# Two of 22 down-projection chunks as whole float32 products in a hybrid encoder trunk

## The chip, the cores and the metric

The kernel runs on one core of a Trainium2 chip, in one launch. The metric is the device time of an execution in microseconds; where several executions were timed, it is their median. The kernel before took 907.94 us, the median of three runs from 906.53 to 909.02 us.

## What is computed

The reference is a trunk of two macaron layers over 256 tokens of width 1024, all in float32. Each layer has a feed-forward network (FFN), a mixer (an mLSTM in the first layer, a windowed attention in the second) and a second FFN, each followed by a layer norm:

```python
def swiglu(x, w_in, w_out):
    gu = x @ w_in
    g, u = gu[..., :D_FF], gu[..., D_FF:]
    return (jax.nn.silu(g) * u) @ w_out

for l in range(DEPTH):                                   # DEPTH = 2
    x = layer_norm(ALPHA * x + 0.5 * swiglu(x, ffn_w_in[l, 0], ffn_w_out[l, 0]), ...)
    y = mlstm_mixer(x, ...) if l % 2 == 0 else window_attention(x, ...)
    x = layer_norm(ALPHA * x + y, ...)
    x = layer_norm(ALPHA * x + 0.5 * swiglu(x, ffn_w_in[l, 1], ffn_w_out[l, 1]), ...)
```

`D_FF` is 2816, so the hidden vector h = silu(g) * u of an FFN is 22 chunks of 128 features, and the down product h @ w_out is a sum over these 22 chunks.

## The kernel before

**Split operands.** Nearly every matmul runs on operands of type float32r. A weight tile of 128 x 1024 float32 arrives by DMA as a word (`w_raw`, or `s_raw` for sums of blocks). ScalarE casts it to a high part (`w_hi`, in `Weights.high`, L299), VectorE subtracts that from the word for a low part (`w_lo`, in `Weights.low`). Activations are split likewise (`h_hi`, `h_lo`; `xT`). A product is then three parts: high by high, low by high and high by low (`HH`, `LH`, `HL`, `mm_by`). VectorE, ScalarE and TensorE thus all have a share of each word.

**An FFN.** Chunks 0 to 3 of h come from wide products and are turned by TensorE transposes (`tr`, L817), which write to a PSUM bank and are read from there by ScalarE and VectorE. Chunks 4 and 5 come from narrow products that have the weights as the standing operand, so that their h lies turned already, in `v[1]`, a tile of 128 x 512 float32. `turn` splits it into `hp[0]` (ScalarE) and `hp[1]` (VectorE). Chunks 6 to 21 come from four runs of `seven` (L973), which forms two by two blocks with seven products instead of eight and needs sums of weight blocks for that.

**The down product.** `down(n)` (L942) takes the next n words of w_out and adds their chunk to four PSUM banks, y[t][o], two blocks of 128 tokens by two halves of 512 columns. A chunk is twelve matmuls of 512 columns: three parts by four banks. In the first run of `seven`, chunk 4 follows the product with S4, and chunk 5 the product after it.

**What sets the order.** TensorE's order is the order of the program text. What VectorE and ScalarE do between is set by `Paced`, a recording layer that keeps a clock for each engine from simple costs, and by `Weights.fill` (L375), which splits the next words whenever these clocks say that VectorE or ScalarE is idle. `Paced.on_tensor` (L160) counts a float32 matmul as two passes. Loads stand in SyncE's queue in the order in which `Weights.load` (L222) issued them; a load needs a free room. There are four rooms of the tag `w_raw` and one more inside an FFN, and a room comes free when the word's low part has been made (`Weights.drop`, L260). Up to ten high and ten low parts are kept (`RING`).

**The mLSTM.** After the projections of q and k come, for each of four heads, `scores` (L1230; VectorE weighs the scores in `wt`, ScalarE casts them to `a_hi`, VectorE makes `a_lo`) and, one head later, `mix` (L1249), whose first matmul needs `a_hi`. Between them stand products for the output gate with eight words, taken at once by `W.take(8)` (L1321). Ahead of that, `W.done(most=1 if m and g else 2)` (L1223) lets one more word be split.

Of the kernel before, what the change touches and what calls it, by code (L numbers as in the profile page):

```python
# [9 lines left out]
F32 = mybir.dt.float32  # L10
# [32 lines left out]
PEND = [6, 4, 6, 6, 6]  # L43


AHEAD = 300.0
URGENT = 3
SOON = -1000.0
# [139 lines left out]
class Weights:  # L188
# [110 lines left out]
    def high(self, i):  # L299

        nc = self.nc
        p = self.plan[i]
        while self.half and (p["word"] not in self.raw or any(h[0] == p["needs"] for h in self.half)):
            self.low()
        while any(s_[0] == p["needs"] or p["word"] not in self.raw for s_ in self.sums):
            self.sum()
        if p["word"] not in self.raw:
            return False
        scale, raw = p["scale"], self.raw[p["word"]]
        hi = self.pool.tile([128, D], FR, name="w_hi", tag="w_hi", bufs=RING)  # L310
        if i == 0:
            for j in range(2):
                s_ = slice(j * 512, j * 512 + 512)
                nc.scalar.copy(hi[:, s_], raw[:, s_])
        elif scale is None:
            nc.scalar.copy(hi, raw)
        else:
            nc.scalar.activation(hi, raw, AF.Copy, scale=scale())
        self.half.append((i, hi))
        self.made.add(i)  # L320
        return True
# [82 lines left out]
    def take(self, n):  # L404
# [2 lines left out]
        self.split(self.used)  # L407
        return [self.parts[j] for j in range(i, i + n)]

    def take_rows(self, n):  # L410
        return [(self.used + j, w) for j, w in enumerate(self.take(n), -n)]

# [34 lines left out]
def trunk_kernel(ctx: ExitStack, tc: tile.TileContext, x, ffn_w_in, ffn_w_out, ln_g, ln_b, ml_w_in, ml_gate_b,  # L447
# [17 lines left out]

    clock = [0.0]

    def split_of(w, scale=None, needs=None, takes=2720.0, behind=0.0):

        plan.append(dict(word=w, k=words[w]["k"], scale=scale, needs=needs, due=clock[0], behind=behind))  # L470
        clock[0] += takes
        return len(plan) - 1

# [12 lines left out]
    def rows(w, c, scale=None):  # L486
        piece(w[c * 128:(c + 1) * 128, :].rearrange("(k p) f -> p k f", p=128), 1, scale)
# [36 lines left out]
    for j, (kind, l, i, _) in enumerate(stages):  # L524
        if kind == "ffn":
            wi, wo = ffn_w_in[l, i], ffn_w_out[l, i]
            nth = iter(range(2 * UNITS))

            def down(n):
                for _ in range(n):  # L530
                    rows(wo, next(nth))

            for c0 in (0, F):
                for a in range(4):
                    wide(wi, a * 256, c0)
            for c0 in (512, F + 512):
                for a in range(2):
                    narrow(wi, a * 512, c0)
            down(2)
            for g in range(SEVENS):  # L540
                c0 = 768 + 512 * g
                seven(wi, c0, F + c0, g, down)
            down(6)
        elif kind == "mlstm":
            for c0 in (1024, 1536):
                for a in range(4):
                    wide(ml_w_in[0], a * 256, c0)
            for c0 in range(0, 1024, 256):
                for a in range(2):
                    narrow(ml_w_in[0], a * 512, c0)  # L550
            for c0 in (2048, 2560):
                for a in range(4):
                    wide(ml_w_in[0], a * 256, c0)
            for c in range(8):
                rows(ml_w_out[0], c, (lambda c=c: gcol[:, c:c + 1]))
        else:
            for c0 in (1024, 0):
                for a in range(4):
                    wide(at_w_in[0], a * 256, c0)
            for c0 in (512, 768):  # L560
                for a in range(2):
                    narrow(at_w_in[0], a * 512, c0)
            for c in range(8):
                rows(at_w_out[0], c)
        ends[j] = len(words)
# [86 lines left out]
    def wbank(shape=(128, 512)):  # L652
        return psum.tile(list(shape), F32, name="pw", tag="pw", bufs=4)
# [143 lines left out]
    def ffn(l, i, n, pending, last):  # L797
        with ExitStack() as ph:
# [15 lines left out]
                warm(8)  # L814
            hs, pieces = [], []

            def tr(hB, t, h):  # L817
                p = wbank((128, 4, 128))
                for k in range(4):
                    nc.tensor.transpose(p[:, k], h[:, k * 128:(k + 1) * 128], ident)  # L820
                split_evac(pair(hB, A, A, tok(t)), p, wait=True)
# [120 lines left out]
            def down(n_):  # L942
                if not y:
                    y.extend([ybank() for _ in range(2)] for _ in range(2))
                W.flush()
                for _ in range(n_):
                    c = done_[0]
                    w, = W.take(1)
                    mm_by([((0, 1), [HH, LH]), ((2, 3), [HH]), ((0, 1, 2, 3), [HL]), ((2, 3), [LH])],
                          [(y[t][o], pair(hT[c], A, tok(t)), pair(w, A, 0, slice(o * 512, o * 512 + 512)), c == 0, False)  # L950
                           for t in range(2) for o in range(2)])
                    W.done()
                    done_[0] += 1
# [88 lines left out]
            for m in range(2):  # L1042
                p = [wbank((128, 2, S)) for _ in range(2)]
                for a in range(2):
                    w, = W.take(1)
                    for c in range(2):
                        for k in range(4):
                            nc.tensor.matmul(p[c], w[0][:, k, tok(c)], x_both[:, :, 4 * a + k], start=a == k == 0,
                                             stop=False)
                    for c in range(2):  # L1050
                        for k in range(4):
                            nc.tensor.matmul(p[c][:, 1], w[1][:, k, tok(c)], xT[0][:, 4 * a + k], start=False,
                                             stop=a == 1 and k == 3)
                        if a:
                            summed(p[c], v[m], c)
                    W.done()
                    if not start:
                        for n_, f_ in zip(XP[1:], (x_three, x_two, x_four)):
                            if 2 * m + a == n_:
                                f_()  # L1060
                    if m and not a:
                        W.flush()
                        for t in range(0 if start else 1, 2):
                            tr(hB0, t, hs[t])
                        nc.scalar.activation(v[0], v[0], AF.Silu)
            W.when_ready(lambda: nc.vector.tensor_mul(v[1], v[0], v[1]))
            chunks(hp, 2)
            down(1)

            def turn():  # L1070
                W.flush()
                nc.scalar.copy(hp[0], v[1])
                W.when_ready(lambda: nc.vector.tensor_sub(hp[1], v[1], hp[0].bitcast(F32)), hp[0])

            down(1)
            for g in range(SEVENS):
# [12 lines left out]
    def mlstm(l, n, pending, last):  # L1089
        with ExitStack() as ph:  # L1090
# [121 lines left out]
            for m in range(2):  # L1212
                for g in range(2):
                    pieces = W.take(2)
                    for f in range(2):
                        p = wbank((128, 2, S))
                        for k in range(8):
                            mm_both(p, pair(pieces[k // 4], A, k % 4, tok(f)), k, k == 0, k == 7)
                        if m == g == f == 0:
                            turn_gates()  # L1220
                        split_both(pair(held["qk"[m]], A, 2 * g + f), p, 128 ** -0.5 if m else 1.0,
                                   tile_([128, S], F32, "left"))
                    W.done(most=1 if m and g else 2)  # L1223
                    weights(2 * m + g)
                    W.done(0, 0 if m and g else 1)

# [91 lines left out]

            pump = iter(MP)
            spare = lambda: W.done(0, next(pump))  # L1320
            pieces = W.take(8)  # L1321
            po = [wbank(), wbank()]
            for h in range(4):
                wide_mm(po[h // 2], 0, pieces, h // 2, range(4 * (h % 2), 4 * (h % 2) + 4))
                if h > 1:
                    spare()
                scores(h, (lambda: combine(h - 2)) if h > 1 else None)
                if h == 0:
                    nc.scalar.preload_act_table(AF.Sigmoid)
                if h == 3:  # L1330
                    held.clear()
                    wt.clear()
                    for tag in TAGS[1:]:
                        W.back(tag, S_RAW)
                if h:
                    mix(h - 1)
                    divide(h - 1, (lambda: settle(h - 2)) if h > 1 else None)
                if h > 1:
                    spare()
# [299 lines left out]
```

## Time and profile before

| | us |
|---|---|
| median of three runs (lowest, highest) | 907.94 (906.53, 909.02) |
| the profiled execution's own time | 907.99 |
| its span, from the first to the last instruction | 906.2 |
| TensorE busy | 895.4 |
| VectorE busy | 809.3 |
| ScalarE busy | 573.0 |
| GpSimd busy | 144.1 |

The profiled execution is one run; 1.8 us of its time lie around the span. A row of a group gives the line, the engine (PE is TensorE, DVE VectorE, ACT ScalarE, POOL GpSimd, SP SyncE, with a q for an engine's queue), the operation, the output and inputs by their names in the program, the shapes, the count, the busy time and the mean length of one in nanoseconds, then the idle time ahead of them and what ended it. For a matmul the moving operand stands first behind the arrow and the standing one second. Nearly all instructions show line 179, the recording layer's call, so that groups are told by their tiles. Matmuls overlap: their starts are measured, their ends modelled.

### The profile page before, as it was taken

How to read it: one execution, taken by the hardware profiler on the slowest of the kernel's cores; microseconds unless marked ns; L12 is line 12 of the kernel's file. 1: busy time of each engine (PE TensorE's matmuls, PEld its weight loads, DVE VectorE, ACT ScalarE, POOL GpSimd, SP SyncE). 2: the span in 40 equal slices, each digit the busy share in tenths (PEclk: the TensorE clock that was granted, in tenths of full speed). 3: DMA queues.
4: the chain of work that ended last, by engine and by line, in shares of the span. 5: the costliest groups of instructions: out<-in, count | busy, mean ns of one | idle time of the engine just before them, and what ended most of it. 6: DMA issues, size and time to landing. Idle time of an engine off the chain costs nothing.

```text
span 906.2 us, 12409 instructions
## 1 busy us (share of the span) xinstructions
PE 895.4 (99%) x4403; PEld 748.5 (83%) x4403; DVE 809.3 (89%) x995; ACT 573.0 (63%) x798; POOL 144.1 (16%) x177
## 2 busy tenths in 40 slices
PE   9999999999999999999999999999999999999996
PEld 8888888888888888888888888888887788888885
DVE  5999999878799899999988999998867899899985
ACT  4876777447664666767636676765568566676760
POOL 0111113113221011211111112110413110111110
PEclk9999999999999999999999999999999999999998
DMA  8999998545637889998868899987333687999851
GB/s 280 356 291 292 309 258 213 186 141 165 225 94 243 321 213 243 298 265 248 242 203 288 216 279 289 281 212 231 120 112 117 238 274 241 226 300 265 244 140 46
DMA packets 100477, 208.53 MB, mean 230 GB/s; under 512 B 6664, under 2 KB 21040, under 8 KB 100416
## 3 DMA queue, kind: packets, MB, share of 16 engines
q1 hardware_dynamic: 82112, 173.04, 54.7%
q0 software_dynamic: 17728, 33.66, 22.4%
q10 hardware_dynamic: 576, 1.05, 0.4%
q8 instruction: 34, 0.56, 0.3%
q14 instruction: 27, 0.22, 0.1%
HBM read 206.65 MB, written 1.05 MB: 229 GB/s over the span
## 4 chain that ended last, share of the span: by engine, by line
PE 90%; DVE 4%; DMA 2%; issue 2%; ACT 2%; DVEq 0%; POOL 0%; POOLq 0%
PE pw L179 54%; PE py L179 35%; DVE w_lo L179 2%; DMA w_raw<-in_ml_w_in_dram 1%; DMA w_raw<-in_ffn_w_in_dram 1%; ACT w_hi L179 1%; DVE scan L179 1%; ACT wt L179 0%; DVE x L179 0%; DMA both_rows<-both_rows 0%; DVE left L179 0%; DVE stats L179 0%; DVE S_lo L179 0%; DVE s_raw L179 0%; DVE S L179 0%
## 5 line engine op out<-in xcount | busy, mean ns | idle before, releaser
L179 DVE TENSOR_TENSOR w_lo<-w_raw,w_hi 128x1024 fp32r<-128x1024 f32 (+1 forms) x213 | 255.5, 1219 | 20.2 <-ACT w_hi L179 18.7
L179 ACT CAST w_hi<-w_raw 128x1024 fp32r<-128x1024 f32 (+1 forms) x213 | 219.0, 1050 | 70.0 <-DMA w_raw<-in_ffn_w_in_dram 18.3
L179 DVE TENSOR_TENSOR w_lo<-s_raw,w_hi 128x1024 fp32r<-128x1024 f32 x192 | 228.8, 1217 | 12.2 <-ACT w_hi L179 12.2
L179 ACT CAST w_hi<-s_raw 128x1024 fp32r<-128x1024 f32 x192 | 196.2, 1053 | 66.1 <-DVE s_raw L179 41.5
L179 PE MATMUL pw<-w_hi,xT 128*128 128x512 f32 x832 | 236.8, 393 | 0.0
L179 PEld LDWEIGHTS pw<-w_hi,xT 128*128 128x128 f32 x832 | 154.5, 188 | 31.2 <-DVE xT L179 0.3
L120 POOL DMA_DIRECT2D s_raw<-in_ffn_w_in_dram x64 | 77.4, 1209 | 484.0 <-DVE s_raw L179 211.1
L179 PE MATMUL pw<-w_lo,xT 128*128 128x512 f32 x416 | 136.1, 390 | 0.0
L179 PE MATMUL py<-w_hi,h_hi 128*128 128x512 f32 x349 | 117.3, 396 | 0.0
L179 PE MATMUL py<-w_hi,h_lo 128*128 128x512 f32 x349 | 115.3, 390 | 0.0
L179 PE MATMUL py<-w_lo,h_hi 128*128 128x512 f32 x349 | 104.8, 390 | 0.0
L179 PEld LDWEIGHTS pw<-w_lo,xT 128*128 128x128 f32 x416 | 78.1, 188 | 16.3
L179 PE MATMUL pw<-w_lo,S_hi 128*128 128x512 f32 x256 | 78.8, 389 | 0.0
L179 PE MATMUL pw<-w_hi,S_hi 128*128 128x512 f32 x256 | 78.8, 389 | 0.0
L179 PE MATMUL pw<-w_hi,S_lo 128*128 128x512 f32 x256 | 78.8, 389 | 0.0
L179 DVE TENSOR_TENSOR s_raw<-s_raw,s_raw 128x1024 f32<-128x1024 f32 x64 | 76.8, 1219 | 0.5
L179 PEld LDWEIGHTS py<-w_hi,h_lo 128*128 128x128 f32 x349 | 65.5, 188 | 14.0
L179 PEld LDWEIGHTS py<-w_lo,h_hi 128*128 128x128 f32 x349 | 65.6, 188 | 13.5
L179 PEld LDWEIGHTS py<-w_hi,h_hi 128*128 128x128 f32 x349 | 64.4, 188 | 12.2
L179 ACT COPY e<-pw 128x512 f32<-128x512 f32 (+1 forms) x64 | 33.7, 534 | 37.5 <-PE pw L179 36.8
L179 PEld LDWEIGHTS pw<-w_hi,S_hi 128*128 128x128 f32 x256 | 48.1, 188 | 10.0
L179 PEld LDWEIGHTS pw<-w_lo,S_hi 128*128 128x128 f32 x256 | 48.1, 188 | 10.0
(197 smaller groups left out, 1065.6 us busy)
## 6 DMA issues: line engine op xcount, KB each, us to landing
s_raw<-in_ffn_w_in_dram SPq DMA_DIRECT2D x96, 512.0 KB, 8.0
w_raw<-in_ffn_w_out_dram SPq DMA_DIRECT2D x88, 512.0 KB, 6.3
w_raw<-in_ffn_w_in_dram SPq DMA_DIRECT2D x80, 512.0 KB, 5.8
s_raw<-in_ffn_w_in_dram POOLq DMA_DIRECT2D x64, 512.0 KB, 8.1
w_raw<-in_ml_w_in_dram SPq DMA_DIRECT2D x24, 512.0 KB, 4.6
w_raw<-in_at_w_in_dram SPq DMA_DIRECT2D x12, 512.0 KB, 4.5
w_raw<-in_ml_w_out_dram SPq DMA_DIRECT2D x8, 512.0 KB, 3.9
w_raw<-in_at_w_out_dram SPq DMA_DIRECT2D x8, 512.0 KB, 3.4
```

The lines of the kernel that those rows point to most:

```text
L120: self.nc.gpsimd.dma_start(ap, source, accum_op=OP.add)
L179: r = f(out, *args, **kw)
```

## The change

The change does four things.

- **Chunks 4 and 5 in one product.** `WHOLE = (4, 5)` names them. Their words are not split; the raw word itself is the moving operand, and h stays one float32 tile, written by VectorE's multiplication straight into the room of `hp[0]`. A chunk is now four matmuls with float32 operands. The split of h in `turn` is gone. The word's room comes free only when these four matmuls are done.
- **Two transposes' banks.** In the first FFN the two calls of `tr` inside the narrow products take their bank from the `py` banks, not from the `pw` banks.
- **A word's split.** In the mLSTM, `W.done` ahead of the last head's weights splits no word (`most=0`), and of the eight words for the output gate seven are taken at first and the eighth behind the first call of `scores`.
- **Bookkeeping** for these: `take_whole`, a field `whole` in the plan.

```diff
@@ Weights.high
+        if p["whole"]:
+            self.parts[i] = raw
+            self.made.add(i)
+            return True
@@ Weights
+    def take_whole(self):
+        w, = self.take(1)
+        return self.plan[self.used - 1]["word"], w
@@ ffn: tr
-            def tr(hB, t, h):
-                p = wbank((128, 4, 128))
+            def tr(hB, t, h, bank=wbank):
+                p = bank((128, 4, 128))
@@ ffn: down
+                    if c in WHOLE:
+                        i, w = W.take_whole()
+                        for t in range(2):
+                            for o in range(2):
+                                nc.tensor.matmul(y[t][o], whole[:, c - WHOLE[0], tok(t)], w[:, o * 512:o * 512 + 512],
+                                                 start=False, stop=False)
+                        W.drop(i)
+                        W.load()
+                        W.done()
+                        done_[0] += 1
+                        continue
@@ ffn: narrow products
-                            tr(hB0, t, hs[t])
+                            tr(hB0, t, hs[t], ybank if start else wbank)
-            W.when_ready(lambda: nc.vector.tensor_mul(v[1], v[0], v[1]))
+            whole = hp[0].bitcast(F32)
+            W.when_ready(lambda: nc.vector.tensor_mul(whole, v[0], v[1]))
@@ ffn: turn
-                nc.scalar.copy(hp[0], v[1])
-                W.when_ready(lambda: nc.vector.tensor_sub(hp[1], v[1], hp[0].bitcast(F32)), hp[0])
@@ mlstm
-                    W.done(most=1 if m and g else 2)
+                    W.done(most=0 if m and g else 2)
@@ mlstm
-            pieces = W.take(8)
+            pieces = W.take(7)
...
                 scores(h, (lambda: combine(h - 2)) if h > 1 else None)
+                if h == 0:
+                    pieces.extend(W.take(1))
```

On TensorE, in the first FFN, this is the place from the end of the product with S4 over chunk 4 to the product behind it, before:

```order
L179 MATMUL pw<-w_lo,S_hi 128x512 x2
L179 MATMUL py<-w_hi,h_hi 128x512 x2
L179 MATMUL py<-w_hi,h_lo 128x512 x2
L179 MATMUL py<-w_hi,h_hi 128x512 x2
L179 MATMUL py<-w_lo,h_hi 128x512 x4
L179 MATMUL py<-w_hi,h_lo 128x512 x2
L179 MATMUL pw<-w_hi,xT 128x512 x4
```

The same place after the change, on to chunk 5 (`h_hi` is now the room that holds the whole h):

```order
L180 MATMUL pw<-w_lo,S_hi 128x512 x2
L180 MATMUL py<-w_raw,h_hi 128x512 x4
L180 MATMUL pw<-w_hi,xT 128x512 x4
L180 MATMUL pw<-w_lo,xT 128x512 x2
L180 MATMUL pw<-w_hi,xT 128x512 x4
L180 MATMUL pw<-w_lo,xT 128x512 x2
L180 MATMUL pw<-ident,e_674 128x128 x4
L180 MATMUL py<-w_raw,h_hi 128x512 x4
```

Twelve instructions became four for each of the two chunks; nothing else moved on this engine.

On VectorE, in the mLSTM, these rows lead from the last head's k to the second head's scores, before:

```order
L179 SCALAR_TENSOR_TENSOR k_lo<-pw,left 128x256
L179 TENSOR_TENSOR w_lo<-w_raw,w_hi 128x1024
L179 TENSOR_TENSOR wt<-pw,wt 128x2x256
L179 TENSOR_TENSOR wt<-pw,wt 128x2x128
L179 TENSOR_TENSOR a_lo<-wt,a_hi 128x768
L179 TENSOR_TENSOR wt<-pw,wt 128x2x256
```

And after:

```order
L180 SCALAR_TENSOR_TENSOR k_lo<-pw,left 128x256
L180 TENSOR_TENSOR wt<-pw,wt 128x2x256
L180 TENSOR_TENSOR wt<-pw,wt 128x2x128
L180 TENSOR_TENSOR a_lo<-wt,a_hi 128x768
L180 TENSOR_TENSOR w_lo<-w_raw,w_hi 128x1024
L180 TENSOR_TENSOR wt<-pw,wt 128x2x256
```

One low part moved behind the first head's `wt` and `a_lo`; its cast on ScalarE moved in the same way.

In SyncE's queue, in the second FFN, the loads around chunks 4 and 5, with what each waits for, before:

```order
L116 DMA w_raw_3361<-in_ffn_w_out_dram 128x1024 [waits DMAHW6_49,DVE_49]
L116 DMA w_raw_3408<-in_ffn_w_out_dram 128x1024 [waits DMAHW7_49,DVE_49]
L116 DMA w_raw_3449<-in_ffn_w_in_dram 128x2x512 [waits DMAHW0_49,DVE_49]
L116 DMA w_raw_3460<-in_ffn_w_in_dram 128x2x512 [waits DMAHW1_49,DVE_49]
L116 DMA s_raw0_3471<-in_ffn_w_in_dram 128x2x512 [waits DMAHW2_49,DMASW4_49]
L116 DMA s_raw0_3497<-in_ffn_w_in_dram 128x2x512 [waits DMAHW3_49,DMASW5_49]
L116 DMA w_raw_3524<-in_ffn_w_out_dram 128x1024 [waits DMAHW5_49,DMAHW4_49,DVE_49]
L116 DMA s_raw1_3542<-in_ffn_w_in_dram 128x2x512 [waits DMASW6_49,DVE_49]
```

And after:

```order
L117 DMA w_raw_3401<-in_ffn_w_out_dram 128x1024 [waits DMAHW6_49,DVE_49]
L117 DMA w_raw_3405<-in_ffn_w_out_dram 128x1024 [waits DMAHW7_49,PE_49]
L117 DMA w_raw_3413<-in_ffn_w_in_dram 128x2x512 [waits DMAHW0_49,DVE_49]
L117 DMA s_raw0_3424<-in_ffn_w_in_dram 128x2x512 [waits DMAHW1_49,DMASW4_49]
L117 DMA s_raw0_3449<-in_ffn_w_in_dram 128x2x512 [waits DMAHW2_49,DMASW5_49]
L117 DMA w_raw_3451<-in_ffn_w_in_dram 128x2x512 [waits DMAHW3_49,PE_49]
L117 DMA w_raw_3478<-in_ffn_w_out_dram 128x1024 [waits DMAHW5_49,DMAHW4_49,DVE_49]
L117 DMA s_raw1_3491<-in_ffn_w_in_dram 128x2x512 [waits DMASW6_49,DVE_49]
```

Two loads that waited for VectorE now wait for TensorE, for the rooms of chunks 4 and 5, and one of them moved behind two loads of `s_raw`.

More of the change, by code (lines that the diff above doesn't have):

```diff
@@ L43 @@
 PEND = [6, 4, 6, 6, 6]
+WHOLE = (4, 5)
 AHEAD = 300.0
@@ L466, in trunk_kernel, with split_of @@
     clock = [0.0]
-    def split_of(w, scale=None, needs=None, takes=2720.0, behind=0.0):
-        plan.append(dict(word=w, k=words[w]["k"], scale=scale, needs=needs, due=clock[0], behind=behind))
+    def split_of(w, scale=None, needs=None, takes=2720.0, behind=0.0, whole=False):
+        plan.append(dict(word=w, k=words[w]["k"], scale=scale, needs=needs, due=clock[0], behind=behind,
+                         whole=whole))
         clock[0] += takes
@@ L530, in down @@
                 for _ in range(n):
-                    rows(wo, next(nth))
+                    c = next(nth)
+                    if c in WHOLE:
+                        split_of(word(wo[c * 128:(c + 1) * 128, :].rearrange("(k p) f -> p k f", p=128), 1), whole=True)
+                    else:
+                        rows(wo, c)
             for c0 in (0, F):
@@ L947, in down @@
                     c = done_[0]
+                    if c in WHOLE:
+                        i, w = W.take_whole()
[8 more added lines that the diff above has]
+                        continue
                     w, = W.take(1)
```

## Prediction

> **What bounds the kernel now.** I read the page's first part, then TensorE's waits, then the stretches of time of the four FFNs, then the timeline at each place that the change touches.
>
> ```profile
> span 906.2 us, 12409 instructions
> PE 895.4 (99%) x4403; PEld 748.5 (83%) x4403; DVE 809.3 (89%) x995; ACT 573.0 (63%) x798; POOL 144.1 (16%) x177
> ```
>
> ```profile
> PE py L179 <- DVE ident L179: 1.7, 1, 1.7
> PE py L179 <- ACT a_hi L179: 1.0, 1, 1.0
> PE pw L179 <- DVE e L179: 0.7, 1, 0.7
> ```
>
> These three rows are all the waits that the trace shows on TensorE: 1.7 us at the start, 1.0 for `a_hi` in the mLSTM, 0.7 for `e` in the first FFN. The stretches (length, then each engine's busy time) say the same of the FFNs, here the second, and the end of the span:
>
> ```profile
> 290.00:450.00 160.00, 160.00 (x744) 133.21 (x743) 150.27 (x157) 108.18 (x131) 20.93 (x17) 1.00 0.92 264
> ...
> 895.00:906.00 11.00, 3.94 (x26) 3.42 (x25) 6.76 (x14) 0.00 (x0) 0.92 (x1) 0.78 0.25 95
> ```
>
> TensorE is busy in all of the FFN, at a granted clock of 1.00. VectorE is close behind, at 150 of 160 us, but nothing waits for it there. So the time of this kernel is the length of TensorE's work, plus 11.0 - 3.9 = 7 us at the end and the three waits. What VectorE or ScalarE is spared inside an FFN brings nothing by itself.
>
> **Chunks 4 and 5, as they are.** Chunk 4 of the first FFN on TensorE (start, length, count):
>
> ```profile
> 70.40 0.62 PE L179 MATMUL py<-w_hi,h_hi 128*128 128x512 f32 x2
> ...
> 73.12 0.39 PE L179 MATMUL pw<-w_hi,xT 128*128 128x512 f32 x1
> ```
>
> From 70.40 to 73.12 are 2.72 us for twelve matmuls: 0.227 each, for 512 columns.
>
> **What a float32 matmul costs.** One place in the trace has such matmuls that are not transposes: the attention's products of `pr` and v. There are eight in a call, each of 256 columns, on one half of the array's columns (64), the halves in turn. The profile's groups, with the nearest split matmuls and the float32 transposes:
>
> ```profile
> L179 PE MATMUL py<-w_lo,h_hi 128*128 128x512 f32 x349 | 104.8, 390 | 0.0
> L179 PE MATMUL pw<-ident,e 128*128 128x128 f32 x128 | 19.1, 272 | 0.0
> L179 PE MATMUL pw<-pr,v 128*64 128x256 f32 x64 | 7.8, 385 | 0.0
> L179 PE MATMUL py<-v_lo,a_hi 128*128 128x258 f32 x24 | 6.3, 282 | 0.0
> ```
>
> The first call in time, seen up to 681.15 us and up to 681.18, then whole:
>
> ```profile
> 680.90 0.44 PE L179 MATMUL pw<-pr,v 128*64 128x256 f32 x2
> 680.90 0.65 PE L179 MATMUL pw<-pr,v 128*64 128x256 f32 x4
> 680.90 1.95 PE L179 MATMUL pw<-pr,v 128*64 128x256 f32 x16
> ```
>
> Eight matmuls are 16 records, so each float32 matmul is two passes. They start in pairs: two by 681.15, and the next two by 681.18. A pair is one pass of each half, side by side, and each further pair adds (1.95 - 0.44) / 7 = 0.216 us, for 256 columns. A split matmul of 512 columns takes 0.227. So a float32 pass moves a column in twice the time, and there are two passes: four times a split part. The mean lengths agree: from 258 to 512 columns a split matmul grows from 282 to 390 ns, 0.425 ns a column, and a float32 pass of 256 columns lasts 385, as long as 500 columns would.
>
> A whole chunk is four matmuls of two passes of 512 columns, each pass 2 x 0.216 = 0.431 us: 8 x 0.431 = 3.45 us in place of 2.72. That is **+0.73 us a chunk, and with eight chunks +5.9 us**, all of it on TensorE, which sets the end. The ends: a pass of exactly 0.42 us (twice the smallest step shown, 0.65 - 0.44 = 0.21) gives 3.36 and +5.1; a pass of two full split matmuls, 0.454, gives 3.63 and +7.3. I take the middle value because it is read from the same kind of instruction. No wait hides any of it, as there is none in these stretches.
>
> The Trainium skill, FP8 and Floating Point Precision, TensorE Precision Notes, speaks against this change: true float32 is four passes through the array, high and low parts of both operands by each other, where the three split parts leave out low by low. The trace agrees as to the price, but shows it as two records of double length. By that rule alone, four passes at 0.227 us, the sum would be the upper end, +7.3.
>
> **The split that goes.** Per chunk a low part on VectorE and a cast on ScalarE, and per FFN the smaller split of h:
>
> ```profile
> L179 DVE TENSOR_TENSOR w_lo<-w_raw,w_hi 128x1024 fp32r<-128x1024 f32 x211 | 254.3, 1224 | 20.2 <-ACT w_hi L179 18.7
> ```
>
> ```profile
> L179 ACT CAST w_hi<-w_raw 128x1024 fp32r<-128x1024 f32 x211 | 217.9, 1054 | 68.8 <-PE py L179 17.6 <-DMA w_raw<-in_ffn_w_in_dram 17.1 <-PE pw L179 12.9
> ```
>
> In two chunks of four FFNs VectorE is spared 8 x 1.22 = 9.8 us, ScalarE 8 x 1.05 = 8.4, without the split of h. TensorE's own work, 160.00 of 160 us, covers all of it: neither engine is waited for there, so this is **0**. Only if VectorE set the pace of these stretches would up to 9.8 us come back. The multiplication that makes h is the same as before and only writes to another room, so it is 0 too.
>
> **The two transposes' banks.** In the first FFN:
>
> ```profile
> 39.45 1.09 PE L179 MATMUL pw<-ident,hh 128*128 128x128 f32 x8 [0.70 <-DVE e L179]
> ...
> 43.65 0.62 PE L179 MATMUL py<-w_hi,h_lo 128*128 128x512 f32 x2
> ```
>
> ```profile
> 33.24 1.27 DVE L179 TENSOR_TENSOR hh<-sg,pw 128x512 f32<-128x512 f32 x2
> ...
> 38.98 0.74 DVE L179 TENSOR_TENSOR e<-e,pw 128x256 f32<-128x256 f32 x2
> ...
> 41.92 1.28 DVE L179 TENSOR_TENSOR h_lo<-pw,h_hi 128x512 fp32r<-128x512 f32 x2
> ```
>
> The data, `hh`, was there at 34.5; the wait was for `e` to be read out of the bank. With a free `py` bank it goes: **-0.7 us**. What is late next is `h_lo`: VectorE is busy without a gap here, so the first of the two still ends near 41.92 + 0.64 = 42.6, and its first user moves from 43.65 to 42.95. That fits, but by 0.4 us only, so I bound this between 0 and -0.7.
>
> **The split in the mLSTM.** VectorE, ScalarE and TensorE there:
>
> ```profile
> 236.38 1.22 DVE L179 TENSOR_TENSOR w_lo<-w_raw,w_hi 128x1024 fp32r<-128x1024 f32 x1
> 237.51 1.01 DVE L179 TENSOR_TENSOR wt<-pw,wt 128x512 f32<-128x512 f32 x2
> ```
>
> ```profile
> 238.56 0.83 ACT L179 CAST a_hi<-wt 128x768 fp32r<-128x768 f32 x1 [1.75 <-DVE wt L179]
> ```
>
> ```profile
> 238.20 0.28 PE L179 MATMUL pw<-q_hi,k_lo 128*128 128x256 f32 x1
> 239.53 0.36 PE L179 MATMUL py<-v_hi,a_hi 128*128 128x258 f32 x1 [1.05 <-ACT a_hi L179]
> ```
>
> The chain is low part, `wt`, `a_hi`, `mix`. Without the low part ahead, `wt` starts 237.51 - 236.38 = 1.13 us sooner and `mix` at 239.53 - 1.13 = 238.40, just as TensorE comes free: **-1.1 us**. The moved low part then delays the second head's `wt` by nothing, as the two exchange places. The bounds are 0 (another wait takes its place) and -1.3, all that lies between TensorE's two starts, 238.20 and 239.53.
>
> **The sum.** Against the profiled execution's own time, 907.99 us (span 906.2 and 1.8 around it): 907.99 + 5.9 - 0.7 - 1.1 = 912.1. The median of the runs is 907.94, the same within 0.05, so I say **912.0 us**. At the ends of the costs it is 907.9 + 5.1 - 0.7 - 1.3 = 911.0 and 907.9 + 7.3 = 915.2. About 0.3%, 2.7 us, is what a measurement of this kernel can tell from no change: 905.2 to 910.7 counts as the same.
>
> **The rivals.** *A float32 pass at full width is a pass at full speed* (ends faster). The pairs of `pr` matmuls read two streams at once, one for each half of the array; if that is what halves their pace, a whole matmul has two passes of 0.227 us. `Paced` counts it so. A chunk is then 8 x 0.227 = 1.82 us, -0.9, eight chunks -7.2, and the time 907.9 - 7.2 - 1.8 = 898.9. The chunk's cost turns at 2.72 / 8 = 0.34 us a pass. Against it stand the transposes: full width, float32, 128 columns, 272 ns. A split matmul of 128 columns would last 282 - 130 x 0.425 = 227; the transposes' 45 ns more are 106 more columns, again nearly double. Transposes may be a case of their own. 0.08.
>
> *The waits take more than I gave them* (no change). If passes are at the lower end and both waits return all that lies in them, the sum is its lower end, 911.0, just outside 910.7; the scatter of the runs (906.53 to 909.02 before) can bring such a kernel's median to 910. For it speaks only that each term may be a little off in the same direction. 0.13.
>
> *Held rooms stall the loads* (slower still). A whole word keeps its room until its matmuls end, and SyncE's queue holds the next load until then, with `s_raw` loads behind it. In the second FFN chunks 4 and 5 began on TensorE, and SyncE's queue went:
>
> ```profile
> 352.56 0.62 PE L179 MATMUL py<-w_hi,h_hi 128*128 128x512 f32 x2
> ...
> 358.36 0.71 PE L179 MATMUL py<-w_hi,h_hi 128*128 128x512 f32 x2
> ```
>
> ```profile
> 343.28 8.99 SPq L116 DMA_DIRECT2D w_raw<-in_ffn_w_out_dram  x3
> 357.27 1.56 SPq L116 DMA_DIRECT2D w_raw<-in_ffn_w_in_dram  x2
> 358.93 1.81 SPq L116 DMA_DIRECT2D s_raw<-in_ffn_w_in_dram  x2
> 365.29 0.34 SPq L116 DMA_DIRECT2D w_raw<-in_ffn_w_out_dram  x1
> ```
>
> At 3.45 us a chunk, chunk 4 there ends near 356.0 and chunk 5 near 358.36 + 0.73 + 3.45 = 362.5. The third of the three loads, sent near 343.28 + 8.99 = 352, waits to 356, and the second `w_in` load to 362.5, but the `s_raw` pair that stood at 358.93 now goes ahead of that one, and the next loads stood at 365.29 anyway. Three of five rooms go on. So I expect no stall; one of 4 us, the delay of that third load, in one FFN gives 916.0, and it decides only where a word lands after its turn on TensorE. 0.06.
>
> **How the numbers follow.** The forecast has 0.73, 912.0 us. Faster by over 0.3%: 0.08, the first rival alone. Within 0.3%: 0.13. Slower by over 0.3%: 0.73 + 0.06 = 0.79. The range runs from 909.3, inside the no-change case, to 916.0, the stalled case; left out are the first rival and the far ends.
>
> **What would show it.** Right: the group `py<-w_raw,h_hi` has 64 records and a chunk takes 3.4 to 3.6 us from its first start to the next group's start; TensorE's waits for `e` and `a_hi` are gone or under 0.2 us; VectorE is busy at least 9.8 us less, and TensorE is as good as always busy in the FFNs, as before. Wrong: a chunk of 1.8 us, or TensorE waits for words or for `h_lo` in an FFN.

## The result and the profile after

The changed kernel's median is 913.46 us (912.92 to 913.95, 3 runs), beside 907.94 before: ratio 1.0063, 95% interval 1.005 to 1.0077. It is slower by 5.5 us. Run again beside 21 runs of the kernel before (median 907.08), it took 913.47 us, ratio 1.007 (1.0058 to 1.0083): slower by 6.4 us, with an interval from 5.3 to 7.5. The forecast was 912.0.

The profiled execution took 912.92 us. The page's span and its busy times:

```profile
span 910.7 us, 12300 instructions
PE 901.2 (99%) x4371; PEld 742.0 (81%) x4371; DVE 799.0 (88%) x983; ACT 561.5 (62%) x786; POOL 143.2 (16%) x177
```

TensorE is busy 5.8 us longer with 32 records fewer. VectorE is spared 10.3 us and ScalarE 11.5, and the kernel is slower all the same. All of TensorE's waits in this trace, and the second FFN and the last stretch (length, busy time of each engine, granted clock):

```profile
PE py L180 <- DVE ident L180: 1.7, 1, 1.7
PE pw L180 <- DVE w_lo L180: 0.8, 1, 0.8
```

```profile
290.00:450.00 160.00, 160.00 (x729) 130.53 (x729) 146.52 (x152) 103.97 (x127) 20.96 (x17) 1.00 0.91 263
899.00:911.00 12.00, 4.75 (x30) 4.12 (x28) 7.56 (x15) 0.00 (x0) 0.92 (x1) 0.83 0.23 87
```

The waits for `e` and `a_hi` are gone, and one for a `w_lo` is new. TensorE is still never idle in the second FFN; VectorE's work there fell from 150.27 to 146.52 us, and that brought nothing. The end is as before. The group of the whole chunks, and chunk 4 of the first FFN on the timeline of TensorE (start, length, count):

```profile
L180 PE MATMUL py<-w_raw,h_hi 128*128 128x512 f32 x64 | 28.8, 592 | 0.0
```

```profile
69.40 3.59 PE L180 MATMUL py<-w_raw,h_hi 128*128 128x512 f32 x8
72.43 1.48 PE L180 MATMUL pw<-w_hi,xT 128*128 128x512 f32 x4
73.75 0.62 PE L180 MATMUL pw<-w_lo,xT 128*128 128x512 f32 x2
```

The four matmuls of the chunk are 8 records, and 64 in all for the eight chunks. Their lengths overlap with what follows, so I count from start to start: the row at 72.43 shows its first matmul's length drawn out while the last pass ends, so I go back from the start behind it, 73.75 less four split matmuls of 0.227. The chunk ends at 72.84 and lasted 72.84 - 69.40 = 3.44 us, 0.430 a pass. Before it was 2.72: **+0.72 us a chunk**, and +5.8 for eight.

The two places of the moves on TensorE, the turns of `hh` in the first FFN and the first head's `mix` in the mLSTM:

```profile
38.50 1.03 PE L180 MATMUL py<-ident,hh 128*128 128x128 f32 x8
...
238.64 0.28 PE L180 MATMUL pw<-q_hi,k_lo 128*128 128x256 f32 x1
238.76 0.28 PE L180 MATMUL py<-v_hi,a_hi 128*128 128x258 f32 x1
```

Both start without a wait, 0.95 and 0.77 us sooner than before (39.45 and 239.53), though two whole chunks, +1.4 us, lie between them. Of the 0.95, only 0.08 us is an earlier arrival: the last products ahead of the turns begin at 37.55 us, and at 37.63 before. So this pair of traces holds the gains that I forecast: their times differ by 4.9 us, of which 4.5 lie in the span and 0.4 around it (2.2 us around the span in place of 1.8, in the medians of later runs too; why is not shown). The medians differ by 5.5 and 6.4. The changed kernel took the same time twice, and the kernel before was 0.9 us faster in its 21 runs than in its first three. Of 57 later runs of the kernel before, 53 were faster than the profiled execution's 907.99 us. The gap between the pair of traces and the medians is what the experiments are about.

### The profile page after: what moved, and what is told of

Its sections match the earlier page's. It is cut to its first block, busy times and chain, and to the rows that moved or that the text cites. A ratio compares the mean times of both kernels' runs of the same rounds, so it can differ in the third digit from the quotient of the medians.

```text
span 910.7 us, 12300 instructions
## 1 busy us (share of the span) xinstructions
PE 901.2 (99%) x4371; PEld 742.0 (81%) x4371; DVE 799.0 (88%) x983; ACT 561.5 (62%) x786; POOL 143.2 (16%) x177
## 3 DMA queue, kind: packets, MB, share of 16 engines
q10 hardware_dynamic: 576, 1.05, 0.4%
HBM read 206.65 MB, written 1.05 MB: 228 GB/s over the span
## 4 chain that ended last, share of the span: by engine, by line
PE 96%; DVE 2%; DMA 1%; issue 0%; ACT 0%; DVEq 0%; POOL 0%; POOLq 0%
PE pw L180 61%; PE py L180 35%; DVE w_lo L180 1%; DMA s_raw<-in_ffn_w_in_dram 1%; DVE x L180 0%; DVE stats L180 0%; DVE e L180 0%; DVE s_raw L180 0%; DVE h_lo L180 0%; DVE pr L180 0%; DVEq L1661 0%; DVE q_lo L180 0%; ACT h_hi L180 0%; ACT e L180 0%; DVE mv L180 0%
## 5 line engine op out<-in xcount | busy, mean ns | idle before, releaser
L180 DVE TENSOR_TENSOR w_lo<-w_raw,w_hi 128x1024 fp32r<-128x1024 f32 (+1 forms) x205 | 246.3, 1221 | 18.7 <-ACT w_hi L180 16.9
L180 ACT CAST w_hi<-w_raw 128x1024 fp32r<-128x1024 f32 (+1 forms) x205 | 210.5, 1050 | 65.8 <-DMA w_raw<-in_ffn_w_in_dram 20.4
L180 PE MATMUL pw<-w_hi,xT 128*128 128x512 f32 x832 | 240.0, 396 | 0.0
L180 PE MATMUL py<-w_hi,h_hi 128*128 128x512 f32 x317 | 107.1, 395 | 0.0
L180 PE MATMUL py<-w_hi,h_lo 128*128 128x512 f32 x317 | 105.4, 390 | 0.0
L180 PE MATMUL py<-w_lo,h_hi 128*128 128x512 f32 x317 | 96.2, 389 | 0.0
L180 PEld LDWEIGHTS py<-w_hi,h_lo 128*128 128x128 f32 x317 | 59.5, 188 | 12.7
L180 PEld LDWEIGHTS py<-w_lo,h_hi 128*128 128x128 f32 x317 | 59.6, 188 | 12.2
L180 PEld LDWEIGHTS py<-w_hi,h_hi 128*128 128x128 f32 x317 | 58.7, 188 | 11.2
L180 PEld LDWEIGHTS pw<-w_hi,S_lo 128*128 128x128 f32 x256 | 48.1, 188 | 10.0
```

The lines of the kernel that those rows point to most:

```text
L180: r = f(out, *args, **kw)
```

## The experiments

After the result my theory was the forecast's sum: the float32 passes make the loss, and each wait removed is time gained. The first four runs were made to test its terms, against the rivals that the moves are worth nothing and that VectorE or the loads set the pace. As to the moves it fell, and I formed theory A: the two removed waits only took up lateness that TensorE has in most runs anyway, so removing them is worth little in the median. In the runs on the moves after that, B is the forecast's view, and C that the moves cost elsewhere what they gain.

### Both moves without the whole chunks

`WHOLE`, `take_whole` and the changed `turn` are left out; the rest of the change stands.

```diff
-            def tr(hB, t, h):
-                p = wbank((128, 4, 128))
+            def tr(hB, t, h, bank=wbank):
+                p = bank((128, 4, 128))
...
-                            tr(hB0, t, hs[t])
+                            tr(hB0, t, hs[t], ybank if start else wbank)
...
-                    W.done(most=1 if m and g else 2)
+                    W.done(most=0 if m and g else 2)
...
-            pieces = W.take(8)
+            pieces = W.take(7)
...
+                if h == 0:
+                    pieces.extend(W.take(1))
```

> Chunks 4 and 5 split as before; the two transposes' banks and the mLSTM's split moved as in the change. If the float32 price on TensorE is what made the change slower, the two moves alone are worth the two waits, 0.95 and 1.2 us by TensorE's starts: ratio to before 0.9977, about 905.8 us, and TensorE waits neither for e nor for a_hi. If the moves only shift the waits elsewhere, no change, 1.000.

Measured: 907.51 us (906.11 to 908.73, 11 runs) beside 907.41 (15 runs), ratio 1.0003 (0.9994 to 1.0012). The moves are worth between -0.5 and +1.1 us. The profiled run was the fastest of the eleven, span 904.3, and its trace has one wait only:

```profile
PE py L179 <- DVE ident L179: 1.7, 1, 1.7
```

So one run shows the whole gain, and the median, where 905.8 was expected, none of it. The spans of the eleven runs lie between 904.3 and 907.0, those of the 15 runs of the kernel before between 904.8 and 906.0.

### The whole chunks without the moves

The change, with the moves above taken back.

> Chunks 4 and 5 whole; both moves undone. If TensorE's price is the cause: eight chunks of 3.44 us for 2.72, +5.8 us, with the two old waits back: ratio 1.0064 to 1.0074 (the upper one if the new wait of 0.9 us for a low part in the fourth FFN is there too), 913.7 to 914.7 us. If the new wait for low parts and held rooms weigh more than TensorE's price, waits on TensorE add up to over 3 us in its profile.

Measured: 913.67 us (913.63 to 913.76, 5 runs), ratio 1.0069 (1.0057 to 1.0082). That is 0.2 us from the changed kernel with its moves. All waits of TensorE in its trace, and three of TensorE's rows near its start:

```profile
PE py L180 <- DVE ident L180: 1.7, 1, 1.7
PE pw L180 <- DVE w_lo L180: 0.8, 1, 0.8
PE py L180 <- DMA x<-in_x_dram: 0.5, 1, 0.5
```

```profile
5.42 1.11 PE L180 MATMUL py<-ident,x 128*128 128x128 f32 x4 [0.45 <-DMA x<-in_x_dram]
6.32 1.21 PE L180 MATMUL py<-ident 128*128 128x128 f32 x8
7.41 0.70 PE L180 MATMUL pw<-w_hi,xT 128*128 128x512 f32 x2
```

The waits for `e` and `a_hi` are not in this list, though the code that had them is back. TensorE came to both places later: it began its products with x at 7.41 us, where the trace of before has 6.97 (below), and the first FFN's whole chunks added 1.4 us ahead of the mLSTM. Of `a_hi` a little is left: `mix` starts 0.41 us after the product ahead of it (239.42 and 239.83 us), and 0.12 us after it in the changed kernel. Of what the moves remove, about 0.3 us was there to be removed.

### One whole chunk in place of two

Chunk 4 whole, chunk 5 split as before, both moves kept. h of chunk 4 is written to a tile of its own, `hw`.

```diff
-WHOLE = (4, 5)
+WHOLE = (4,)
...
+            whole = pool.tile([128, 1, S], F32, name="hw", tag="hw", bufs=1)
...
```

> Only chunk 4 whole, chunk 5 split as before; both moves kept. TensorE's price counts by chunk: four chunks of +0.72 us are +2.9, the moves -2.1: ratio 1.0008, about 908.7 us, no new wait. If one held room suffices to stall the loads, a wait for a low part stays in a later FFN and the ratio is 1.002.

Measured: 910.41 us (909.89 to 910.8, 5 runs), ratio 1.0033 (1.002 to 1.0046), +3.0 us. Its group:

```profile
L180 PE MATMUL py<-w_raw,hw 128*128 128x512 f32 x32 | 14.4, 592 | 0.0
```

Four chunks at +0.72 are +2.9, and the measured +3.0 leaves nothing for the moves; 908.7 was expected. Its trace has no wait for a low part. The price per chunk stands; the gain of the moves fails here too.

### The high parts alone

Chunks 4 and 5 with only high by high; the other two products are left out, but all parts are still made. Both moves kept.

```diff
-                    mm_by([((0, 1), [HH, LH]), ((2, 3), [HH]), ((0, 1, 2, 3), [HL]), ((2, 3), [LH])],
+                    mm_by([((0, 1, 2, 3), [HH])] if c in (4, 5) else
+                          [((0, 1), [HH, LH]), ((2, 3), [HH]), ((0, 1, 2, 3), [HL]), ((2, 3), [LH])],
```

> Chunks 4 and 5 take only their high by high part, four split matmuls of 0.227 us; low by high and high by low of these chunks are left out, while both parts are still made. Both moves kept. If TensorE's length is the time in these stretches, eight chunks lose 8 x 0.227 = 1.82 us each: -14.5 us, and with the moves -16.6: ratio 0.9817, about 891.3 us. If VectorE, busy 150 of 160 us in an FFN, sets the pace as soon as TensorE is shorter, the ratio stays above 0.987 and TensorE shows waits for low parts of several us in each FFN.

Measured: 913.09 us (911.75 to 914.25, 5 runs), ratio 1.0062 (1.0049 to 1.0074). With 64 matmuls, 14.5 us of TensorE's work, less, it is slower than before. The page's busy times and TensorE's waits:

```profile
PE 887.1 (97%) x4339; PEld 738.0 (81%) x4339; DVE 809.5 (89%) x995; ACT 571.3 (63%) x798; POOL 143.4 (16%) x177
```

```profile
PE pw L179 <- DVE w_lo L179: 14.3, 8, 2.8
PE py L179 <- DVE ident L179: 1.7, 1, 1.7
PE py L179 <- ACT h L179: 0.6, 1, 0.6
PE py L179 <- DMA x<-in_x_dram: 0.5, 1, 0.5
```

Eight waits for a `w_lo`, two in each FFN and 14.3 us in all, take the place of the 14.5 us: the expectation's second theory held. So the splits that I called covered are covered by very little where these chunks stand; the planner's order, which shifts with these matmuls too, is not held apart from it. Whether the first rival's shorter chunk would have met the same waits is not shown, as its own word needs no split.

The granted clock was 0.988 to 0.995 in these runs (0.997 to 0.999 before). In the trace it is 0.50 in two stretches within the FFNs (length, busy time of each engine, granted clock):

```profile
385.90:389.30 3.40, 2.87 (x7) 1.77 (x7) 3.40 (x4) 0.00 (x0) 0.00 (x0) 0.50 1.09 273
563.40:570.20 6.80, 5.58 (x16) 3.97 (x15) 6.29 (x8) 2.81 (x4) 0.00 (x0) 0.50 1.07 324
```

Each begins within 1 us of the end of one of the eight waits, of 2.01 us (up to 385.83) and of 2.45 us (up to 562.48). TensorE's 8.45 us of busy time in them at half the clock cost some 4 us, an estimate. With the waits this outweighs the 14.5 us. Why the clock fell behind these two waits and not behind those of 2.35 and 2.76 us is not shown.

### Each move by itself

The bank alone, and the split alone, in the kernel before.

> The kernel before with one edit: the first FFN's two turns of the high half go to y's banks instead of w's. The wait of TensorE for e (0.70 us) is not there any more. Theory A (the wait only takes up lateness that TensorE has anyway in most runs, since x's loads come at other times): 907.2 to 907.6 beside 907.4 of the kernel before. Theory B (the forecast's: each wait removed is time gained): 906.7. Theory C (the move itself costs something later, a bank that comes free late): above 907.8, with a new wait of TensorE in the trace.

> The kernel before with one edit: one word's split is moved in the mLSTM, out of the four that follow the key product and behind the first scores. The wait of TensorE for a_hi (1.05 us) is not there any more, that for e (0.7 us) still is. Theory A (the wait only takes up lateness): 907.0 to 907.6. Theory B (each wait removed is time gained): 906.3. Theory C (the moved split costs as much elsewhere): 907.4 or more, with a wait for w_lo or w_hi in the mLSTM or the FFN behind it.

Measured: the bank 907.42 us (906.41 to 908.12, 11 runs), ratio 1.0002 (0.9993 to 1.001); the split 907.53 (906.68 to 909.47, 11 runs), ratio 1.0003 (0.9994 to 1.0012); 907.19 before (21 runs). B's gains, 0.7 for the bank and 1.1 for the split, lie outside the intervals (down to -0.6 and -0.5), the first by little. The second text expected the wait for `e` to stay, and it is not in that trace, although the banks are the old ones: `e` was read by 39.21 us and TensorE came to the turns at 39.26. In the same trace, TensorE at the third head:

```profile
249.53 0.28 PE L179 MATMUL pw<-q_hi,k_lo 128*128 128x256 f32 x1
250.27 0.39 PE L179 MATMUL py<-v_hi,a_hi 128*128 128x258 f32 x1 [0.45 <-ACT h L179]
```

Here is a wait that before did not have, 0.45 us for ScalarE's `h`, in a later step of the same mLSTM: part of what C says, though on another tile than it named. The first `mix` starts 1.09 us sooner than before (238.44 and 239.53), but that `h` comes hardly sooner. ScalarE before, and with the split alone:

```profile
250.00 0.84 ACT L179 ACTIVATE h<-py,den 128x256 f32<-128x256 f32 x2 [1.20 <-DVE den L179]
```

```profile
249.74 0.84 ACT L179 ACTIVATE h<-py,den 128x256 f32<-128x256 f32 x2 [1.20 <-DVE den L179]
```

It is 0.26 us sooner, just as the second head's `wt` is (240.03 us, and 240.29 before), which now has the moved low part ahead of it. So about half of the gain is lost again by the second `mix` (250.27, and 250.83 before). And the list of waits of the bank's trace has the old wait in another size:

```profile
PE py L179 <- ACT a_hi L179: 0.7, 1, 0.7
...
PE py L179 <- DVE h_lo L179: 0.2, 1, 0.2
```

The second row is a wait that before did not have, near the end of the first FFN (167.76 us). The bank's move leaves that place as it was and brings TensorE there sooner (the product ahead starts at 238.04 us, and at 238.20 before), yet the wait is 0.7 us in place of 1.0. So 0.3 us or more of it belonged to the one execution of before that I read.

### Both moves, a second trace

> The kernel before with both moves and its chunks split as before, once more, for a second trace of it. Theory A (without the two waits nothing takes up a late start any more): the time of this run lies above that of the first trace, 906.1, by as much as its first products of x start later than 6.3 us in the trace, to within 0.3 us. Theory B (the scatter comes from elsewhere): the difference appears in a later stage, as idle time of TensorE or as a lower granted clock there.

Measured: 906.88 us in one run, span 905.1. The first products of x on TensorE in the trace of before, in the first of both moves and in this one:

```profile
6.97 0.70 PE L179 MATMUL pw<-w_hi,xT 128*128 128x512 f32 x2
```

```profile
6.29 1.01 PE L179 MATMUL pw<-w_hi,xT 128*128 128x512 f32 x2
```

```profile
6.52 0.71 PE L179 MATMUL pw<-w_hi,xT 128*128 128x512 f32 x2
...
74.95 0.73 PE L179 MATMUL pw<-w_lo,xT 128*128 128x512 f32 x2 [0.52 <-DVE w_lo L179]
```

Same code, 0.8 us longer: 0.23 of it at the start, 0.52 in a wait for a `w_lo` that the first trace does not have. Both theories had a part of it; mine, which gave all of it to the start, missed.

### Nine idle turns ahead of the first wait

Into the kernel before, and into the one with both moves, right ahead of the turns of `hh`, unknown to the planner:

```diff
+                        if start:
+                            idle = ybank((128, 4, 128))
+                            for j in range(9):
+                                nc.nc.tensor.transpose(idle[:, j % 4], ident, ident)
```

> The kernel before with nine idle turns of the identity on TensorE (9 x 0.099 us = 0.9 us of work that nobody uses) in the first FFN, right ahead of the turns of the high half, where the trace of before has TensorE wait 0.70 us for e; nothing else is moved. Theory A (such a wait takes up lateness): the wait for e is gone or under 0.2 us, the turns start 0.1 to 0.4 us later, the later wait for a_hi takes up part of what is left, and the time is 907.2 to 907.6 beside some 907.3 of the kernel before. Theory B (TensorE sets the pace and every addition to its work is paid): 908.2.

> The kernel with both moves and split chunks, with the same nine idle turns at the same place. Theory A (with the two waits gone nothing takes up the 0.9 us any more): 908.2 to 908.5 beside 907.5 of the kernel with both moves, 0.7 or more above the kernel before with the nine turns. Theory C (something behind the first FFN takes it up all the same: VectorE or the loads set the pace of what follows): within 0.3 us of 907.5, with a wait of TensorE that shrinks in the mLSTM or later.

Measured: in the kernel before 907.81 us (907.3 to 909.47, 11 runs), ratio 1.0008 (0.9999 to 1.0017), +0.7; with both moves 908.2 (907.73 to 909.12, 11 runs), ratio 1.001 (1.0001 to 1.0019), +1.1, where they alone had +0.1. With the moves all of the 0.9 us is paid, as A said. Without them most of it is paid too, which is more than A's 0.1 to 0.5, and the interval holds A's figures and B's. A's third figure, 0.7 us or more between the two kernels with the nine turns, failed: it is 0.4. The trace of the first, at the turns:

```profile
38.80 1.15 PE L1066 MATMUL py<-ident 128*128 128x128 f32 x9
39.78 1.04 PE L179 MATMUL pw<-ident,hh 128*128 128x128 f32 x8
```

The turns of `hh` come at 39.78 after nine more turns, and at 39.45 before, with the same start (6.96 and 6.97): 0.33 us of 0.98 is left, and the wait for `e` is gone. But that does not show that the wait took up the addition, as VectorE was ahead in this execution. Its reading of `e`, and ScalarE's cast of a word much earlier:

```profile
38.05 0.75 DVE L179 TENSOR_TENSOR e<-e,pw 128x256 f32<-128x256 f32 x2
```

```profile
17.99 1.05 ACT L179 CAST w_hi<-w_raw 128x1024 fp32r<-128x1024 f32 x1 [1.97 <-DMA w_raw<-in_ffn_w_in_dram]
```

`e` was read by 38.80 us, just when the idle turns began, so that no wait would have come without them either. In the trace of before the same row of VectorE starts at 38.98, and the same cast on ScalarE is later too, as its load landed later:

```profile
19.05 1.05 ACT L179 CAST w_hi<-w_raw 128x1024 fp32r<-128x1024 f32 x1 [2.04 <-DMA w_raw<-in_ffn_w_in_dram]
```

The low part of that word starts at 20.13 us there and at 19.07 here, and VectorE reaches `e` 18.9 and 19.0 us behind it. So when `e` is read goes back to when this load lands.

### The planner's price of a float32 matmul

The changed kernel, with `Paced.on_tensor` counting four passes.

```diff
-        passes = 2.0 if name == "matmul" and ins[0].dtype == F32 else 1.0
+        passes = 4.0 if name == "matmul" and ins[0].dtype == F32 else 1.0
```

> The changed kernel, with one number of its planner altered: a matmul of whole float32 counts as 4 passes of 512 columns instead of 2, so the planner sees a chunk of 3.46 us where the trace shows 3.44, and it orders the splits of words behind it by that. Theory A (the changed kernel's wait of 0.8 us for w_lo in the fourth FFN comes of the planner's too short price): the wait goes, 912.3 to 912.9 beside some 913.4 of the changed kernel. Theory B (the wait comes of rooms that the whole words hold for longer, so that a load of sum words starts late): the wait stays, 913.2 to 913.8. Other orders of splits may bring waits of their own: above 914.

Measured: 912.21 us (911.83 to 913.36, 5 runs), ratio 1.0056 (1.0044 to 1.0069), 0.1 us below A's figures. With the changed kernel on the same chip, once more:

> The changed kernel once more, for its time beside the next kernel on the same chip and for a second trace. Every theory: 913.0 to 913.9, ratio 1.005 to 1.008. If the wait for w_lo in the fourth FFN (0.8 us) belongs to the order of the work, it is there again, within 0.3 us; if it is a chance of the loads, it is not.

> The changed kernel with the planner's price of 4 passes once more, beside the changed kernel. Theory A (the wait for w_lo comes of the planner's too short price of a float32 chunk): 0.7 to 1.2 us below the changed kernel, with no wait for w_lo. Theory B (the first run of it was low by chance): within 0.4 us of it.

Measured: the changed kernel 913.47 us (913.03 to 914.38, 5 runs), ratio 1.007 (1.0058 to 1.0083); with four passes 912.1 (911.36 to 912.43, 5 runs), ratio 1.0056 (1.0042 to 1.0069), 1.4 us less, more than the 0.7 to 1.2 expected, and of these runs none of one kernel lies within the other's (of the five before them with four passes, one took 913.36). The fourth FFN in the changed kernel's first trace: SyncE's queue, VectorE, and TensorE:

```profile
804.39 1.49 SPq L117 DMA_DIRECT2D s_raw<-in_ffn_w_in_dram  x2
809.49 0.34 SPq L117 DMA_DIRECT2D w_raw<-in_ffn_w_out_dram  x1
810.63 1.50 SPq L117 DMA_DIRECT2D s_raw<-in_ffn_w_in_dram  x2
```

```profile
820.58 1.23 DVE L180 TENSOR_TENSOR s_raw<-s_raw,s_raw 128x1024 f32<-128x1024 f32 x1 [0.30 <-DMA s_raw<-in_ffn_w_in_dram]
...
823.05 2.35 DVE L180 TENSOR_TENSOR w_lo<-w_raw,w_hi 128x1024 fp32r<-128x1024 f32 x2
```

```profile
824.78 1.07 PE L180 MATMUL pw<-w_hi,xT 128*128 128x512 f32 x4
826.60 0.50 PE L180 MATMUL pw<-w_lo,xT 128*128 128x512 f32 x1 [0.75 <-DVE w_lo L180]
```

An `s_raw` load lands late, VectorE is idle 0.30 us for it, the low parts behind it in VectorE's row are late, and TensorE waits 0.75 us. The same with four passes (second trace):

```profile
800.36 1.50 SPq L117 DMA_DIRECT2D s_raw<-in_ffn_w_in_dram  x2
806.20 0.34 SPq L117 DMA_DIRECT2D w_raw<-in_ffn_w_out_dram  x1
807.33 1.50 SPq L117 DMA_DIRECT2D s_raw<-in_ffn_w_in_dram  x2
```

```profile
818.78 1.22 DVE L180 TENSOR_TENSOR s_raw<-s_raw,s_raw 128x1024 f32<-128x1024 f32 x1
...
822.38 2.35 DVE L180 TENSOR_TENSOR w_lo<-w_raw,w_hi 128x1024 fp32r<-128x1024 f32 x2
```

```profile
824.42 1.07 PE L180 MATMUL pw<-w_hi,xT 128*128 128x512 f32 x4
825.33 0.62 PE L180 MATMUL pw<-w_lo,xT 128*128 128x512 f32 x2
```

The loads go 3 to 4 us sooner, the sum needs no wait, and TensorE none: from the four `w_hi` products to the next it is 0.91 us from start to start, and 1.82 above. So the wait costs 0.9 us by the starts. The traces with four passes also lack some 0.3 us of delay at the mLSTM's second `mix`. The whole words hold their rooms here as well, so held rooms are not the cause by themselves: the order that the planner made with too low a price is. It remains slower than the kernel before, by 5.0 us; of the kernels tried none is faster than it.

## Why the prediction was right, and where it was not

**What bounds the kernel: right.** VectorE and ScalarE were spared what I said, and more, and TensorE, as good as always busy, left no room for a gain from it; no run spares them alone. **The price of a float32 pass: right**, 0.430 us where I said 0.431, 3.44 a chunk where I said 3.45, and +3.0 us for half of the chunks by the clock. The estimate from the pairs of `pr` and v carried over from 256 columns on half of the array to 512 on the whole; so the first rival, that full width goes at full speed, fell. The Trainium skill, FP8 and Floating Point Precision, TensorE Precision Notes, counts four passes; at 0.227 each they would be 0.91 us per matmul, an estimate, and two records of 0.430 make 0.86. The rule is right as to the size, and the trace decides on the 0.05 us.

**The step that failed** is the sum's "- 0.7 - 1.1" for the two moves. In the pair of traces it is there. In the medians the moves measured +0.1 (-0.5 to +1.1), alone +0.2 and +0.3, and on top of the whole chunks -0.2. I took two waits of one execution, a slow one, for two costs of the kernel. The runs showed this in their place:

- The wait for `e` is the distance between two arrivals, and both differ from execution to execution. TensorE's first products of x begin between 6.29 and 7.75 us in the fourteen traces. VectorE's reading of `e` hangs on the load that lands near 19 us: the low part of that word starts between 18.55 and 20.13 us, and the trace of before is the latest. Of the four traces with the old banks it alone has the wait (one of the others has the idle turns).
- The `a_hi` wait comes in all four traces with the old split, but with 1.05, 0.7, 0.3 and, behind two whole chunks, about 0.3 us by the starts. The moved split does remove it. I had that the moved low part delays the second head's `wt` by nothing, and it does not; but that `wt` hardly comes sooner either, nor does the `h` behind it, and TensorE, now early, waits for `h` at the second `mix` in some traces: 0.45 us with the split alone and 0.35 in the changed kernel's second trace.
- One trace of the moves has a wait of 0.52 us for `w_lo` in the first FFN.

How much of the 1.8 us each of these takes in the usual run stays open: each trace is one execution. My theory A, that TensorE's lateness takes up these waits, is part of it at most, as the idle turns in the kernel before were paid to a larger part than it has it.

**Held rooms:** the loads in the second FFN did what I read from their order. The third load there left at 356 and the second `w_in` load at 362.5:

```profile
349.92 6.25 SPq L117 DMA_DIRECT2D w_raw<-in_ffn_w_out_dram  x3
...
362.45 0.37 SPq L117 DMA_DIRECT2D w_raw<-in_ffn_w_in_dram  x1
```

and nothing waited for them. But I looked at that FFN alone. In the fourth, a late load did reach TensorE, for 0.75 us in one trace and 0.6 in the other, which the sum had at nothing; its rival had 4 us. TensorE waiting for words in an FFN was one of my signs of being wrong. I had quoted that the planner counts two passes, as a point for the first rival, and did not ask what a wrong count does to the order it makes.

Together: 5.8 for the chunks, 0.7 for the new wait, about nothing for the moves are +6.5, and +6.4 (5.3 to 7.5) was measured beside 21 runs. That they meet so closely is partly luck: with four passes, where the wait is gone, +5.0 is left and not 5.8, and 0.4 us of the loss lies outside the span. The forecast's 912.0 came out 1.5 us low, within its range, and its sign for its own reason. Its difference missed by more, +4.1 against +6.4: the 907.9 that it starts from is 0.9 us above the median of the 21 runs, and that hid part of the miss.

## What to carry to other kernels

A wait of a microsecond in one trace is worth that only if the engine comes to it at the same time in every execution: before it goes into a sum, look at it in a second trace, at how far the runs scatter, and at what the engine would wait for next. Where one engine is busy throughout, price a rewrite by its passes on that engine, from start to start, and check at the same time how little cover the others have. A planner that orders loads and splits needs the new operation's true price, or it gives back a part at a place far from the edit.

## What the runs showed of the hardware

A float32 matmul of 512 columns leaves two records of 592 ns mean that start 0.430 us apart; a split one 0.227. The start of the program is not the same from run to run: in nine of the fourteen traces TensorE waited 0.4 to 0.5 us for the load of x, in five not at all, and eight idle turns of the identity right behind took between 1.04 us and 1.62. In the trace with 1.62 they start 0.21 us apart up to 7.4 us and 0.11 us apart from 7.6; in the trace of before that change comes near 6.8. I had not expected 14.5 us less of TensorE's work to end in more time: waits of 14.3 us, and a clock of 0.50 for 10.2 us behind two of them.
